# First stage of a two-layer decoder trunk: distance tables ahead of x, value and key/value weights split by ScalarE and VectorE, sinks on GpSimd

## Chip, cores and metric

One NeuronCore of a Trainium2 chip runs the whole program in one launch. The metric is device time in microseconds (us) of one execution; lower is better. The engines are PE (TensorE matmul; PEld is its weight load), DVE (VectorE), ACT (ScalarE), POOL (GpSimd) and SP (SyncE, which here only issues DMAs).

## What is computed

A trunk of two decoder layers on x of 512 tokens by 1024 channels, in float32. Only the first steps of layer 0 bear on this change:

```python
h = rms_norm(x, g_mix[layer])
proj = jnp.einsum("bsd,de->bse", h, w_in)
aq, ak, av, bq, bk, bv = jnp.split(proj, offs, axis=-1)
aq = rms_norm(aq.reshape(bsz, seq, N_HEADS_A, HEAD_DIM), a_q_gain)
...
a_out = dilated_attention(aq, ak, av, slopes[N_HEADS_B:])
b_out = sliding_window_sink_attention(bq, bk, bv, b_sinks, slopes[:N_HEADS_B])
```

The dilated attention (A, 8 heads) lets token t see the keys at distance 0 to 128, at multiples of 4 up to 512 and at multiples of 16 up to 2048; a key that is in several of these branches counts as often. The sliding window (B, 8 query heads, 2 key/value heads) sees 128 keys and a learned sink per head. Both subtract a slope times the distance. After attention come an output projection and a squared-ReLU MLP, and then layer 1 with another attention.

## The kernel before, in words

Every matmul is made in three products: each float32 operand is split into a high part (whi, h[:, 0]) and a residual (wlo, h[:, 1]), and high times high, residual times high and high times residual are summed in PSUM. A split of weights is one cast (L151 on ScalarE, L153 on GpSimd) and one subtraction (L156 on VectorE or GpSimd). Which engines do it is chosen by a pattern that a counter walks through: PAT_START is ScalarE with VectorE, PAT_ATT is GpSimd with VectorE and then GpSimd for both. The raw weights (wraw) have 4 buffers, whi and wlo 7 each.

A scheduler places the instructions of each engine in one order at build time; an engine runs its own in that order and waits on semaphores. Operations passed through in_order keep the order in which they are written while the start is emitted.

The first stage brings x in by halves. For each of 8 chunks of 128 channels, PE transposes x into a PSUM bank (xT, L629), ScalarE and VectorE write h times the gain and its residual (L160, L161), and ScalarE copies the transposed x to xs, of which GpSimd spills pairs of chunks to DRAM (L641). ScalarE also squares x (junk, L668) for the row statistics. Interleaved with this runs the projection of q and k of the first four A heads, project (L232 to L234), into four PSUM tiles pj0 to pj3. Four banks (pA) serve these projections and the two transposes of gains (pg).

norm_heads then copies each tile to SBUF (qk, L248; these share four buffers with xs), squares it (sq, L250), and VectorE sums the squares per head (ss, L251), takes reciprocal roots in small steps (rsqb, rsq, rs, L130 to L135) and multiplies (L261, shared with GpSimd). In layer 0 sq has a single buffer, which junk and the scratch f of the tables use as well. A PSUM bank is free once both copy and square have read it.

v_a(0) projects the values of the same four heads, 256 columns, 96 matmuls; prep_v scales and splits them (L160, L161). Then attention over A starts: PE transposes q and k (qkT, L268), ScalarE and VectorE split them (L278, L279, L160, L161), a DMA on SP swaps halves of K (L291), and scores follow. Interleaved with it run the projections for B: kv_b (256 columns of key and value) and then its queries.

make_tables builds the tables that scores add: dist, the distance; lt, the log of the number of branches; lb, the mask of B. It is emitted after all of the q and k projection. The sinks, negated (nsink, L679), are made on VectorE from a DMA that SP issues behind the weights and the gains.

Of the kernel before, what the change touches and what calls it, by code (L numbers as in the profile page):

```python
# [9 lines left out]
F32 = mybir.dt.float32  # L10
F32R = mybir.dt.float32r
BF16 = mybir.dt.bfloat16
I32 = mybir.dt.int32
# [60 lines left out]
def trunk(ctx, tc, x, g_mix, g_mlp, w_in_even, a_q_gain, a_k_gain, b_q_gain, b_k_gain, b_sinks,  # L74
# [118 lines left out]
    def layer_attention(li, hT, w_in, w_out, stats=None):  # L193


        with ExitStack() as c2:
# [41 lines left out]
                use(outs)  # L238
                yield 0

            def norm_heads(outs, nh):

                w = nh * HD
                qk = [ap.tile([P, 2, 512], F32, tag="qk", bufs=4, name="qk") for _ in range(2)]
                ss = small.tile([P, NT, 8], F32, tag="ss", name="ss")
                for t in range(NT):
                    q = qk[t // 2][:, t % 2, :w]
                    nc.scalar.copy(q, outs[t][:, :w])  # L248
                    sq = ap.tile([P, 512], F32, tag="sq", bufs=1 + li, name="sq")
                    nc.scalar.activation(sq[:, :w], outs[t][:, :w], AF.Square)  # L250
                    nc.vector.reduce_sum(ss[:, t, :nh], sq[:, :w].rearrange("p (h d) -> p h d", d=HD), axis=AX.X)  # L251
                v = small.tile([P, NT, 8], F32, tag="ssv", name="ssv")
                for t in range(NT):
                    nc.vector.tensor_scalar(v[:, t, :nh], ss[:, t, :nh], 1.0 / HD, ecol[:, t:t + 1],
                                            op0=OP.mult, op1=OP.add)
                rs = small.tile([P, NT, 8], F32, tag="rs", name="rs")
                rsqrt_small(rs[:, :, :nh], v[:, :, :nh])
                for t in range(NT):
                    q = qk[t // 2][:, t % 2, :w].rearrange("p (h d) -> p h d", d=HD)
                    eng = nc.gpsimd if NORM[t] == "g" else nc.vector  # L260
                    eng.tensor_mul(q, q, rs[:, t, :nh].unsqueeze(2).to_broadcast([P, nh, HD]))  # L261
                return qk
# [235 lines left out]
                    st["v", g] = prep_v(outs, 0, 4, i)  # L498
                return use

            def qk_use(key, nh):
                def use(outs):
                    st["qk", key] = norm_heads(outs, nh)
                return use

            def all_of(gen):
# [3 lines left out]
            if li == 0:  # L510
# [2 lines left out]
                                   *((PAT_START, True) if g == 0 else ()))  # L513

                def v_a(g):
                    return project([(1024 + g * 256, 1024 + g * 256 + 256)], v_use(g, 0))

                def att_a(g):
                    def get(p_):
# [4 lines left out]
                def kv_b():  # L524
                    def use(outs):
                        st["v", 3] = prep_v(outs, P, 2, 1)
                        st["k", "b"] = norm_heads(outs, 2)
                    return project([(2048, 2304)], use)

                def att_b():  # L530
                    def get(p_):
# [3 lines left out]
                        return prep_q(st["qk", "b"], p_ * P), [k, k]  # L535
                    return attend(get, 0, lambda: st["v", 3], lambda j: j // 4, "b", 0, 4, 4)

                first, qk0 = start(ap, hT), qk_a(0)
                for i, n in enumerate((1, 1 + 8 // GRAIN, 1 + 8 // GRAIN, 1 + 8 // GRAIN)):
                    cnt["start"] = i < STARTPIN  # L540
                    next(first)
                    for _ in range(n):
                        next(qk0)
                cnt["start"] = False
                for _ in range(8 // GRAIN):
                    next(qk0)
                next(first)
                all_of(qk0)
                make_tables(ap, dist, lt, lb)
                all_of(v_a(0))  # L550
                run(att_a(0), 32, chain(kv_b(), project([(1536, 2048)], qk_use("b", 8))), 768, LEADS[0])
                run(att_b(), NB, chain(qk_a(1), v_a(1)), 768, LEADS[1])
# [57 lines left out]
    def start(ap, hT):  # L610
# [65 lines left out]
                                bass.AP(tensor=g.tensor, offset=g.offset, ap=[[HD, 1], [0, 2], [1, HD]]))  # L676
        sink = small.tile([P, HA], F32, tag="sink", name="sink")
        nc.sync.dma_start(sink, bass.AP(tensor=b_sinks.tensor, offset=b_sinks.offset, ap=[[0, P], [1, HA]]))
        nc.vector.tensor_scalar_mul(nsink, sink, -1.0)  # L679
        nc.sync.dma_start(bfor, bass.AP(tensor=b_forget.tensor, offset=b_forget.offset, ap=[[0, P], [1, HC]]))  # L680
        nc.vector.tensor_add(ms[:, 0], ms[:, 0], ms[:, 1])
        col_stats(ms[:, 0])
# [4 lines left out]
    def make_tables(ap, dist, lt, lb):  # L687


        di = ap.tile([P, 512], I32, tag="bias", bufs=2, name="di")  # L690
        nc.gpsimd.iota(di, pattern=[[-1, 512]], base=384, channel_multiplier=1)
        nc.vector.tensor_copy(dist, di)
        mi = ap.tile([P, 512], I32, tag="bias", bufs=2, name="mi")
        mf = mi.bitcast(F32)
        f = ap.tile([P, 512], F32, tag="sq", bufs=1, name="f")
        nc.vector.tensor_scalar(lt, dist, 128.0, None, op0=OP.is_le)
        for m in (3, 15):
            nc.vector.tensor_scalar(mi, di, m, None, op0=OP.bitwise_and)
            nc.vector.tensor_scalar(f, mi, 0.0, None, op0=OP.is_equal)
            nc.vector.tensor_add(lt, lt, f)  # L700
        nc.vector.tensor_scalar(f, dist, 0.0, None, op0=OP.is_ge)
        nc.vector.tensor_mul(lt, lt, f)
        nc.vector.tensor_scalar(f, lt, 0.0, -8.0 * BIG, op0=OP.is_equal, op1=OP.mult)
        for n in (2, 3):
            nc.vector.tensor_scalar(mf, lt, float(n), float(8 * np.log(n)), op0=OP.is_equal, op1=OP.mult)
            nc.vector.tensor_add(f, f, mf)
        nc.vector.tensor_copy(lt, f)
        nc.vector.tensor_scalar(f[:, :256], dist[:, 256:], 0.0, -8.0 * BIG, op0=OP.is_lt, op1=OP.mult)
        nc.vector.tensor_scalar(lb, dist[:, 256:], 128.0, -8.0 * BIG, op0=OP.is_ge, op1=OP.mult)
        nc.vector.tensor_add(lb, lb, f[:, :256])  # L710

    def forget(ap, outs):

# [439 lines left out]
```

## Time and profile before

| | us |
|---|---|
| median of 3 runs | 1192.4 |
| lowest and highest run | 1188.94, 1193.04 |
| profiled execution, its own time | 1192.98 |
| span in its trace | 1191.2 |
| busy in the span: PE, PEld | 1162.3, 1020.3 |
| busy: VectorE, ScalarE, GpSimd | 893.1, 646.0, 212.1 |
| PE on the chain that ended last | 81% |

The span runs from the first to the last instruction; the execution's time has some 2 us around it. PE is busy for 98% of the span, so what counts is where PE waits, and for whom. A busy PE can still be slow: the granted clock says at which share of full speed it ran. A row of the timeline gives start, duration, engine, line, operation and tiles, and in brackets the idle time before it with what ended it. Durations of neighbours overlap a little, since instructions are pipelined; the distance between two starts is the better measure of a pace.

### The profile page before, as it was taken

What the parts mean: (1) busy time and instruction counts of PE and PEld (TensorE: products, weight loads), DVE (VectorE), ACT (ScalarE), POOL (GpSimd) and SP (SyncE); (2) the same over time, 40 slices, a digit from 0 to 9 for tenths busy, and PEclk for the clock granted to TensorE, in tenths of its full rate; (3) what the DMA queues carried; (4) which work ended last, traced back from release to release, by engine and by line L of the source; (5) the groups of instructions that cost most, each with busy time, mean ns of one, the idle gap of its engine ahead of it and who ended that gap; (6) DMA issues with size and microseconds to landing.
All of it is one profiled execution on the core that took longest, in us unless ns stands there. A gap on an engine that the chain in (4) does not pass through costs nothing.

```text
span 1191.2 us, 18927 instructions
## 1 busy us (share of the span) xinstructions
PE 1162.3 (98%) x6902; PEld 1020.3 (86%) x6902; DVE 893.1 (75%) x1962; ACT 646.0 (54%) x1351; POOL 212.1 (18%) x307
## 2 busy tenths in 40 slices
PE   8799989999999999999999999999999999999998
PEld 7787887888888988988887888887889989889897
DVE  4987899878956947865657887878879578569585
ACT  6255876665445545444335675655655455455453
POOL 2445444200000000000155445432000000000000
PEclk9899999999999999999999999999999999999999
DMA  7342115232332332233443433343322423323322
GB/s 250 114 109 79 37 37 155 76 103 75 107 110 84 94 120 88 90 113 109 152 125 107 106 100 100 103 124 106 107 89 72 125 89 106 103 83 100 116 68 82
DMA packets 106197, 122.46 MB, mean 103 GB/s; under 512 B 6088, under 2 KB 95208, under 8 KB 106104
## 3 DMA queue, kind: packets, MB, share of 16 engines
q1 hardware_dynamic: 104920, 117.03, 32.3%
q0 software_dynamic: 576, 2.10, 0.5%
q10 hardware_dynamic: 608, 2.13, 0.4%
q8 instruction: 54, 0.88, 0.3%
q14 instruction: 39, 0.32, 0.1%
HBM read 108.10 MB, written 6.32 MB: 96 GB/s over the span
## 4 chain that ended last, share of the span: by engine, by line
PE 81%; DVE 10%; DMA 3%; issue 2%; ACT 2%; POOL 1%; SPq 0%; ACTq 0%; POOLq 0%; DVEq 0%
PE up L165 10%; PE up L168 10%; PE up L169 10%; PE pj L232 4%; PE pj L234 4%; PE pj L233 4%; PE Y L950 3%; PE Y L953 3%; PE Y L954 3%; PE O L383 2%; PE Z L950 2%; PE X L953 2%; PE X L950 2%; PE Z L954 2%; PE Z L953 2%; PE X L954 2%
## 5 line engine op out<-in xcount | busy, mean ns | idle before, releaser
L165 PE MATMUL up<-xin,whi 128*128 128x512 f32 x512 | 199.8, 390 | 0.0
L168 PE MATMUL up<-xin,wlo 128*128 128x512 f32 x512 | 199.3, 389 | 0.0
L169 PE MATMUL up<-xin,whi 128*128 128x512 f32 x512 | 199.2, 389 | 0.0
L763 ACT CAST whi<-wraw 128x512 fp32r<-128x512 f32 (+1 forms) x228 | 138.7, 613 | 106.4 <-PE up L169 48.3
L764 DVE TENSOR_TENSOR wlo<-wraw,whi 128x512 fp32r<-128x512 f32 (+1 forms) x228 | 152.1, 679 | 56.5 <-ACT whi L763 54.3
L169 PEld LDWEIGHTS up<-xin,whi 128*128 128x128 f32 x512 | 96.1, 188 | 20.1
L165 PEld LDWEIGHTS up<-xin,whi 128*128 128x128 f32 x512 | 96.1, 188 | 20.0 <-issue 0.2
L168 PEld LDWEIGHTS up<-xin,wlo 128*128 128x128 f32 x512 | 96.1, 188 | 19.9 <-issue 0.2
L763 ACT CAST whi<-s 128x512 fp32r<-128x512 f32 (+1 forms) x112 | 67.6, 604 | 70.0 <-PE Y L954 35.0
L343 ACT ACTIVATE P<-P,negm 128x128 f32<-128x128 f32 (+5 forms) x128 | 69.5, 544 | 52.9 <-DVE negm L340 51.0
L950 PE MATMUL Y<-t,whi 128*128 128x256 f32 x324 | 92.7, 286 | 3.0 <-DVE acc L966 2.6
L901 ACT ACTIVATE u<-up 128x512 f32<-128x512 f32 x64 | 38.3, 598 | 99.7 <-PE up L169 99.7
L953 PE MATMUL Y<-t,wlo 128*128 128x256 f32 x324 | 91.7, 283 | 0.0
L954 PE MATMUL Y<-t,whi 128*128 128x256 f32 x324 | 91.6, 283 | 0.0
L153 POOL TENSOR_SCALAR whi<-wraw 128x512 fp32r<-128x512 f32 x96 | 65.8, 687 | 140.7 <-PE pj L234 118.3
L232 PE MATMUL pj<-whi,hn 128*128 128x512 f32 (+2 forms) x256 | 88.7, 346 | 0.0
L234 PE MATMUL pj<-whi,hn 128*128 128x512 f32 (+2 forms) x256 | 86.9, 339 | 0.0
L233 PE MATMUL pj<-wlo,hn 128*128 128x512 f32 (+2 forms) x256 | 86.8, 339 | 0.0
L764 DVE TENSOR_TENSOR wlo<-s,whi 128x512 fp32r<-128x512 f32 (+1 forms) x112 | 73.7, 663 | 2.4 <-ACT whi L763 2.4
L232 PE MATMUL pj<-whi,h 128*128 128x512 f32 (+1 forms) x192 | 68.5, 361 | 6.9 <-DVE v L161 3.1
L156 POOL TENSOR_TENSOR wlo<-wraw,whi 128x512 fp32r<-128x512 f32 x52 | 69.7, 1344 | 21.8 <-ACT whi L151 18.7
L234 PE MATMUL pj<-whi,h 128*128 128x512 f32 (+1 forms) x192 | 66.6, 348 | 0.0
(200 smaller groups left out, 3138.6 us busy)
## 6 DMA issues: line engine op xcount, KB each, us to landing
wraw<-in_w_up SPq DMA_DIRECT2D x64, 512.0 KB, 3.8
wraw<-in_w_down SPq DMA_DIRECT2D x58, 512.0 KB, 4.0
wraw<-in_w_in_odd SPq DMA_DIRECT2D x36, 256.0 KB, 3.0
K<-K SPq DMA_DIRECT2D x26, 256.0 KB
wraw<-in_w_in_even SPq DMA_DIRECT2D x10, 512.0 KB, 4.4
wraw<-in_w_in_even SPq DMA_DIRECT2D x16, 256.0 KB, 4.4
xl<-xsp SPq DMA_DIRECT2D x8, 512.0 KB
bias<-csp SPq DMA_DIRECT2D x16, 256.0 KB, 3.5
```

Source lines behind the costliest of these rows:

```text
L156: in_order((nc.gpsimd if lo == "pool" else nc.vector).tensor_sub(dst_l, src, dst_h.bitcast(F32)))
L165: m = nc.tensor.matmul(o, wh, xh, start=start, stop=False, skip_group_check=more)
L168: nc.tensor.matmul(o, wl, xh, start=False, stop=False, skip_group_check=more)
L169: nc.tensor.matmul(o, wh, xl, start=False, stop=stop, skip_group_check=more)
L232: nc.tensor.matmul(o, xh, hi[:, :n], start=k == 0, stop=False)
L233: nc.tensor.matmul(o, xh, lo[:, :n], start=False, stop=False)
L234: nc.tensor.matmul(o, xl, hi[:, :n], start=False, stop=k == DC - 1)
L763: sca(nc.scalar.copy(dst_h, src))
L764: late.append(lambda: vec(nc.vector.tensor_sub(dst_l, src, dst_h.bitcast(F32))))
L950: m = nc.tensor.matmul(o, wh, b(0), start=start, stop=False, skip_group_check=more)
L953: nc.tensor.matmul(o, wl, b(0), start=False, stop=False, skip_group_check=more)
L954: nc.tensor.matmul(o, wh, b(1), start=False, stop=stop, skip_group_check=more)
```

## The change

Four edits are in the diff. norm_heads and qk_use get parameters for the tag and the number of buffers of sq. The value projection of the first four A heads and the key/value projection of B take PAT_START. make_tables becomes a generator whose rows keep their written order: ten rows (dist to the first lt) are emitted before x, nine after the first pair of chunks; its scratch f moves from the buffer of sq to that of the probabilities P3. nsink is made by GpSimd.

```diff
-            def norm_heads(outs, nh):
+            def norm_heads(outs, nh, sq_tag="sq", sq_bufs=1 + li):
...
-                    sq = ap.tile([P, 512], F32, tag="sq", bufs=1 + li, name="sq")
+                    sq = ap.tile([P, 512], F32, tag=sq_tag, bufs=sq_bufs, name="sq")
...
-            def qk_use(key, nh):
+            def qk_use(key, nh, *sq):
                 def use(outs):
-                    st["qk", key] = norm_heads(outs, nh)
+                    st["qk", key] = norm_heads(outs, nh, *sq)
...
-                    return project([(1024 + g * 256, 1024 + g * 256 + 256)], v_use(g, 0))
+                    return project([(1024 + g * 256, 1024 + g * 256 + 256)], v_use(g, 0), PAT_START if g == 0 else PAT_ATT)
...
-                    return project([(2048, 2304)], use)
+                    return project([(2048, 2304)], use, PAT_START)
...
-                first, qk0 = start(ap, hT), qk_a(0)
+                tables, first, qk0 = make_tables(ap, dist, lt, lb), start(ap, hT), qk_a(0)
+                next(tables)
                 for i, n in enumerate((1, 1 + 8 // GRAIN, 1 + 8 // GRAIN, 1 + 8 // GRAIN)):
                     cnt["start"] = i < STARTPIN
                     next(first)
                     for _ in range(n):
                         next(qk0)
+                    if i == 0:
+                        next(tables)
...
-                make_tables(ap, dist, lt, lb)
...
-        nc.vector.tensor_scalar_mul(nsink, sink, -1.0)
+        nc.gpsimd.tensor_scalar(nsink, sink, -1.0, 1.0, op0=OP.mult, op1=OP.mult)
...
-        f = ap.tile([P, 512], F32, tag="sq", bufs=1, name="f")
-        nc.vector.tensor_scalar(lt, dist, 128.0, None, op0=OP.is_le)
+        f = scratch(F32, "P3", "f")
+        in_order(nc.vector.tensor_scalar(lt, dist, 128.0, None, op0=OP.is_le))
...
+        yield
...
```

The call of qk_use in qk_a and the one for B's queries are not in the diff: both still read qk_use(g, 8) and qk_use("b", 8).

Three places show what moves. The first is VectorE at the start of the program, before the change:

```order
L692 CAST dist_99<-di_464 128x512 [waits Pool_49]
L698 TENSOR_SCALAR mi_467<-di_464 128x512
L696 TENSOR_SCALAR lt_100<-dist_99 128x512 [waits DVE_49]
L709 TENSOR_SCALAR lb_101<-dist_99 128x256
L624 COPY gcol_83<-pg_140 128x16 [waits PE_49]
L161 SCALAR_TENSOR_TENSOR h0_0_148<-xT_143,gcol_83,h0_0_148 128x512 [waits Activation_49]
L161 SCALAR_TENSOR_TENSOR h0_1_156<-xT_151,gcol_83,h0_1_156 128x512 [waits Activation_49]
L156 TENSOR_TENSOR wlo_167<-wraw_163,whi_166 128x512 [waits DMAHW4_49,DMAHW3_49,Activation_49]
```

and with it, from the last of the first ten table rows on:

```order
L707 TENSOR_TENSOR lt_100<-lt_100,f_110 128x512 [waits DVE_49]
L626 COPY gcol_83<-pg_154 128x16 [waits PE_49]
L161 SCALAR_TENSOR_TENSOR h0_0_162<-xT_157,gcol_83,h0_0_162 128x512 [waits Activation_49]
L161 SCALAR_TENSOR_TENSOR h0_1_170<-xT_165,gcol_83,h0_1_170 128x512 [waits Activation_49]
L156 TENSOR_TENSOR wlo_181<-wraw_177,whi_180 128x512 [waits DMAHW4_49,DMAHW3_49,Activation_49]
L156 TENSOR_TENSOR wlo_185<-wraw_177,whi_184 128x512 [waits Activation_49]
L709 TENSOR_SCALAR f_110<-lt_100 128x512
L711 TENSOR_SCALAR mi_109<-lt_100 128x512
L712 TENSOR_TENSOR f_110<-f_110,mi_109 128x512 [waits DVE_49]
L711 TENSOR_SCALAR mi_109<-lt_100 128x512 [waits DVE_49]
L712 TENSOR_TENSOR f_110<-f_110,mi_109 128x512 [waits DVE_49]
L713 COPY lt_100<-f_110 128x512 [waits DVE_49]
```

Behind the iota's cast three table rows stood ahead of the gains' copy; now nine do, and the other nine stand between the residuals of the first two chunks' weights and the third chunk (three of them below the piece shown).

The second is ScalarE at the end of the first q and k projection, from the last square of x on; "waits" names the engine whose semaphore is awaited. Before:

```order
L668 ACTIVATE junk_385,ms0_135<-x3_109 128x512 [waits Activation_49]
L248 COPY qk_421<-pj0_159 128x512 [waits DMASW0_49,PE_49]
L250 ACTIVATE sq_425<-pj0_159 128x512 [waits Activation_49]
L248 COPY qk_421<-pj1_160 128x512 [waits PE_49]
L250 ACTIVATE sq_429<-pj1_160 128x512 [waits DVE_49]
L248 COPY qk_422<-pj2_161 128x512 [waits DMASW1_49,PE_49]
L250 ACTIVATE sq_433<-pj2_161 128x512 [waits DVE_49]
L248 COPY qk_422<-pj3_162 128x512 [waits PE_49]
L250 ACTIVATE sq_437<-pj3_162 128x512 [waits DVE_49]
L160 ACTIVATE v0_102<-pj0_487,rcol_94 128x4x64 [waits PE_49]
```

and with the change:

```order
L670 ACTIVATE junk_408,ms0_149<-x3_123 128x512 [waits Activation_49]
L248 COPY qk_444<-pj0_173 128x512 [waits DMASW0_49,PE_49]
L250 ACTIVATE sq_448<-pj0_173 128x512 [waits Activation_49]
L248 COPY qk_444<-pj1_174 128x512 [waits PE_49]
L151 CAST whi_555<-wraw_549 128x512
L250 ACTIVATE sq_452<-pj1_174 128x512 [waits DVE_49]
L248 COPY qk_445<-pj2_175 128x512 [waits DMASW1_49,PE_49]
L151 CAST whi_621<-wraw_619 128x512 [waits DMAHW2_49]
L248 COPY qk_445<-pj3_176 128x512 [waits PE_49]
L250 ACTIVATE sq_456<-pj2_175 128x512 [waits DVE_49]
L151 CAST whi_625<-wraw_619 128x512
L151 CAST whi_753<-wraw_751 128x512 [waits DMAHW3_49]
```

The casts of the value weights and of B's key/value weights, which GpSimd made, stand among the head copies and squares; each square after the first still waits for VectorE.

The third is VectorE from the end of the reciprocal roots to the last v residual. Before:

```order
L135 SCALAR_TENSOR_TENSOR rs_445<-rsq_447,rsq_446 128x32 [waits DVE_49]
L161 SCALAR_TENSOR_TENSOR v0_102<-pj0_487,rcol_94,v0_102 128x4x64 [waits Activation_49]
L261 TENSOR_TENSOR qk_421<-qk_421,rs_445 128x512 [waits DMASW0_49,DVE_49]
L261 TENSOR_TENSOR qk_422<-qk_422,rs_445 128x512 [waits DMASW1_49]
L705 TENSOR_SCALAR mi_467<-lt_100 128x512
L161 SCALAR_TENSOR_TENSOR v0_102<-pj1_488,rcol_94,v0_102 128x4x64 [waits Activation_49]
L706 TENSOR_TENSOR f_468<-f_468,mi_467 128x512 [waits DVE_49]
L161 SCALAR_TENSOR_TENSOR v0_102<-pj2_489,rcol_94,v0_102 128x4x64 [waits Activation_49]
L707 COPY lt_100<-f_468 128x512 [waits DVE_49]
L156 TENSOR_TENSOR wlo_910<-wraw_903,whi_909 128x512 [waits DMAHW4_49,Pool_49]
L708 TENSOR_SCALAR f_468<-dist_99 128x256 [waits DVE_49]
L161 SCALAR_TENSOR_TENSOR v0_102<-pj3_490,rcol_94,v0_102 128x4x64 [waits Activation_49]
```

and with the change:

```order
L135 SCALAR_TENSOR_TENSOR rs_468<-rsq_470,rsq_469 128x32 [waits DVE_49]
L261 TENSOR_TENSOR qk_444<-qk_444,rs_468 128x512 [waits DMASW0_49,DVE_49]
L261 TENSOR_TENSOR qk_445<-qk_445,rs_468 128x512 [waits DMASW1_49]
L161 SCALAR_TENSOR_TENSOR v0_102<-pj0_487,rcol_94,v0_102 128x4x64 [waits Activation_49]
L161 SCALAR_TENSOR_TENSOR v0_102<-pj1_488,rcol_94,v0_102 128x4x64 [waits Activation_49]
L161 SCALAR_TENSOR_TENSOR v0_102<-pj2_489,rcol_94,v0_102 128x4x64 [waits Activation_49]
L156 TENSOR_TENSOR wlo_910<-wraw_903,whi_909 128x512 [waits DMAHW4_49,Pool_49]
L161 SCALAR_TENSOR_TENSOR v0_102<-pj3_490,rcol_94,v0_102 128x4x64 [waits Activation_49]
```

The table rows (L705 to L708) are gone from between the q/k products and the v residuals; the products now stand ahead of all four v residuals, and one weight residual ahead of the fourth. After the first two heads of the attention the orders of all engines are the same as before.

## Rows read from the trace of the kernel before

**Rows 1.** Windows: stretch, length, busy PE, PEld, DVE, ACT, POOL, clock, DMA share, GB/s.
```profile
35.30:58.95 23.65, 17.46 (x116) 16.28 (x117) 21.76 (x48) 5.23 (x10) 10.90 (x10) 0.88 0.26 70
```

**Rows 2.** Waits of PE, 0 to 60 us: total, times, longest.
```profile
PE pj L232 <- DVE v L161: 3.1, 3, 2.4
...
PE pj L232 <- POOL wlo L156: 2.3, 1, 2.3
```

**Rows 3.** Timeline of PE: start, us, engine, line, op, out<-in [idle before it <-releaser].
```profile
35.05 0.24 PE L623 MATMUL pg<-ident,rows 22*128 22x22 f32 x1
...
52.09 0.28 PE L233 MATMUL pj<-wlo,h 128*128 128x256 f32 x1
52.21 0.28 PE L234 MATMUL pj<-whi,h 128*128 128x256 f32 x1
...
58.89 0.41 PE L268 MATMUL qkT<-ident,qk 128*128 128x128 f32 x1
```

**Rows 4.** Windows, three short stretches (columns as in rows 1).
```profile
41.00:43.00 2.00, 2.00 (x12) 2.00 (x11) 1.81 (x8) 0.00 (x0) 0.00 (x0) 0.52 0.67 183
58.00:60.00 2.00, 1.92 (x9) 1.92 (x10) 1.64 (x4) 0.66 (x1) 0.00 (x0) 0.50 0.72 205
112.00:116.00 4.00, 2.66 (x14) 1.64 (x12) 3.64 (x6) 0.59 (x1) 3.27 (x3) 1.00 0.91 260
```

**Rows 5.** Timeline of ScalarE, 23 to 38 us.
```profile
23.38 0.63 ACT L668 ACTIVATE junk<-x 128x512 f32<-128x512 f32 x1
...
24.14 0.63 ACT L668 ACTIVATE junk<-x 128x512 f32<-128x512 f32 x1
...
25.91 1.14 ACT L151 CAST whi<-wraw 128x512 fp32r<-128x512 f32 x2
26.94 1.08 ACT L639 COPY xs<-xT 128x512 f32<-128x512 f32 x2
...
36.81 0.60 ACT L250 ACTIVATE sq<-pj 128x512 f32<-128x512 f32 x1 [3.79 <-DVE ss L251]
```

**Rows 6.** Timeline of VectorE, 28 to 59 us.
```profile
28.67 2.76 DVE L681 TENSOR_TENSOR ms<-ms 128x4 f32<-128x4 f32 x1
...
41.18 0.42 DVE L699 TENSOR_SCALAR f<-mi 128x512 f32<-128x512 int32 x1
...
47.60 1.27 DVE L135 SCALAR_TENSOR_TENSOR rsq<-rsq 128x32 f32<-128x32 f32 x1
...
49.58 0.17 DVE L134 TENSOR_TENSOR rsq<-rsq 128x32 f32<-128x32 f32 x1
...
50.79 2.86 DVE L261 TENSOR_TENSOR qk<-qk,rs 128x512 f32<-128x512 f32 x2
...
57.55 0.47 DVE L161 SCALAR_TENSOR_TENSOR v<-pj,rcol,v 128x256 fp32r<-128x256 f32 x1
57.95 0.41 DVE L710 TENSOR_TENSOR lb<-lb,f 128x256 bf16<-128x256 bf16 x1
```

**Rows 7.** Timeline of GpSimd, one row.
```profile
28.95 1.29 POOL L156 TENSOR_TENSOR wlo<-wraw,whi 128x512 fp32r<-128x512 f32 x1
```

**Rows 8.** Timeline of VectorE, first 23 us.
```profile
2.49 0.43 DVE L692 CAST dist<-di 128x512 f16<-128x512 int32 x1 [0.50 <-POOL di L691]
...
5.04 0.17 DVE L624 COPY gcol<-pg 128x16 f32<-128x16 f32 x1 [1.32 <-PE pg L623]
...
12.27 1.28 DVE L156 TENSOR_TENSOR wlo<-wraw,whi 128x512 fp32r<-128x512 f32 x2
20.62 0.17 DVE L679 TENSOR_SCALAR nsink<-sink 128x8 f32<-128x8 f32 x1 [7.06 <-DMA sink<-in_b_sinks]
```

**Rows 9.** Timeline of PE in the dense first stage.
```profile
12.29 0.40 PE L233 MATMUL pj<-wlo,h 128*128 128x512 f32 x1
...
17.95 0.40 PE L233 MATMUL pj<-wlo,h 128*128 128x512 f32 x1
```

**Rows 10.** The spills of x, line 641: time from issue to landing.
```profile
DMA to landing us min/median/max: 3.8/5.2/6.9
```

More of the change, by code (lines that the diff above doesn't have):

```diff
@@ L687, in make_tables, with scratch @@
     def make_tables(ap, dist, lt, lb):
-        di = ap.tile([P, 512], I32, tag="bias", bufs=2, name="di")
+        def scratch(dt, tag, name):
+            return ap.tile([P, 512], dt, tag=tag, bufs=2, name=name)
+        di = scratch(I32, "bias", "di")
         nc.gpsimd.iota(di, pattern=[[-1, 512]], base=384, channel_multiplier=1)
-        nc.vector.tensor_copy(dist, di)
-        mi = ap.tile([P, 512], I32, tag="bias", bufs=2, name="mi")
+        in_order(nc.vector.tensor_copy(dist, di))
+        mi = scratch(I32, "bias", "mi")
@@ L694, in make_tables @@
         mf = mi.bitcast(F32)
-        f = ap.tile([P, 512], F32, tag="sq", bufs=1, name="f")
-        nc.vector.tensor_scalar(lt, dist, 128.0, None, op0=OP.is_le)
+        f = scratch(F32, "P3", "f")
+        in_order(nc.vector.tensor_scalar(lt, dist, 128.0, None, op0=OP.is_le))
         for m in (3, 15):
[L698 to L701, printed above, removed]
@@ L702, in make_tables @@
-        nc.vector.tensor_mul(lt, lt, f)
-        nc.vector.tensor_scalar(f, lt, 0.0, -8.0 * BIG, op0=OP.is_equal, op1=OP.mult)
-        for n in (2, 3):
[L705 to L709, printed above, removed]
@@ L710, in make_tables @@
-        nc.vector.tensor_add(lb, lb, f[:, :256])
+            in_order(nc.vector.tensor_scalar(mi, di, m, None, op0=OP.bitwise_and))
+            in_order(nc.vector.tensor_scalar(f, mi, 0.0, None, op0=OP.is_equal))
+            in_order(nc.vector.tensor_add(lt, lt, f))
+        in_order(nc.vector.tensor_scalar(f, dist, 0.0, None, op0=OP.is_ge))
+        in_order(nc.vector.tensor_mul(lt, lt, f))
+        yield
+        in_order(nc.vector.tensor_scalar(f, lt, 0.0, -8.0 * BIG, op0=OP.is_equal, op1=OP.mult))
@@ new lines, in make_tables @@
+        for n in (2, 3):
+            in_order(nc.vector.tensor_scalar(mf, lt, float(n), float(8 * np.log(n)), op0=OP.is_equal, op1=OP.mult))
+            in_order(nc.vector.tensor_add(f, f, mf))
+        in_order(nc.vector.tensor_copy(lt, f))
+        in_order(nc.vector.tensor_scalar(f[:, :256], dist[:, 256:], 0.0, -8.0 * BIG, op0=OP.is_lt, op1=OP.mult))
+        in_order(nc.vector.tensor_scalar(lb, dist[:, 256:], 128.0, -8.0 * BIG, op0=OP.is_ge, op1=OP.mult))
+        in_order(nc.vector.tensor_add(lb, lb, f[:, :256]))
@@ L712, in forget @@
+        yield
     def forget(ap, outs):
```

## Prediction

> **What bounds the kernel now.** I read the windows by stage first, then the waits of PE, then the timelines of PE, ScalarE and VectorE over the first 60 us. PE is the bound nearly everywhere. The exception that this change can reach is one stretch. From 35.30 to 58.95 us, the first value projection and the hand-over to attention, PE is busy 17.46 of 23.65 us at a mean granted clock of 0.88, while VectorE is busy 21.76 [rows 1]. The waits name above all GpSimd's residual of the value weights (2.3) and VectorE's residual of v (3.1 in three waits, one of 2.4) [rows 2]. The timeline gives the edges: the transpose that ends the dense first stage starts at 35.05 and lasts 0.24, so I count from 35.3; the last value matmul starts at 52.21; the last transpose of q and k starts at 58.89, and I count it to 58.95 [rows 3]. [...] Dense at the upper level a 128x256 matmul follows the last after 0.12 us (52.09 to 52.21 [rows 3]).
>
> **Term 1, the value projection.** It has 96 matmuls, 11.5 us dense, and now ends at 52.3. Its first matmul needs two things: weights and a PSUM bank. The weights came from GpSimd; split by ScalarE and VectorE they are ready near 30, because ScalarE has little to do then. The bank needs the square of the second q/k tile. That square waited 3.79 us, until 36.81, for VectorE's reduction of the first [rows 5], because VectorE sat from 28.67 for 2.76 us in a 128x4 addition while GpSimd made a residual from 28.95 to 30.24 [rows 6, 7]; that work leaves GpSimd here.
>
> The title of the change says two buffers for the squares. The diff does not deliver them: norm_heads and qk_use take a tag and a count, but no caller passes any, so layer 0 keeps one buffer, and the ScalarE order still shows each square from the second on waiting for VectorE. That edit costs and brings nothing, and I count on one buffer.
>
> ScalarE's order: the spill copies of the last chunk end at 28.0 now (26.94 + 1.08) [rows 5]; three of the four squares of x that ran before them move behind, so about 27.1. Then four such squares at 0.76 (23.38 to 24.14) and three casts at 0.57 (1.14 for two) [rows 5] put the first head copy at 31.9. Copy and square end at 33.0, VectorE reduces by 34.0, the second square ends at 34.7: PE starts at once, at 35.3. Its second bank waits for VectorE's copy of the gains, now ahead of the third reduction, about 36.6: 1.3 us idle. The third square ends near 37.0, the fourth near 39.4, when PE has used up 23 of its matmuls: 0.2 idle. End 35.3 + 11.5 + 1.5 = 48.3; I take 48.5, since every link is a sum of rows without slack. **Term 1: -3.8.** Bounds: dense, 46.8 (-5.5); releases and lower clock as now, with only the weights early, 51.2 (-1.1). I take a value nearer the first because 1.5 us of idle is close to what 112 to 116 shows at full clock [rows 4].
>
> Moved to VectorE are four 128x512 residuals (0.64 each, 1.28 for two [rows 8]), to ScalarE eight casts; ScalarE is busy 5.23 us of this stretch [rows 1], so those are covered.
>
> **Term 2, from the last value matmul to the last transpose.** Today 52.3 to 58.95, 6.6 us. The reason is VectorE: 15 table rows, the first at 41.18 and the last at 57.95 [rows 6], some 8 us, lie between the reciprocal roots, the q/k products and the v residuals that PE waits for. They leave. VectorE's new order from the fourth reduction (41.0): a weight residual, then eleven small rows at about 0.2 (0.17 and a gap, 49.58 [rows 6]) = 2.2, plus 1.1 because GpSimd's remaining split falls on them (such a row took 1.27 at 47.60 [rows 6]), so the roots are ready at 45.2. Two products in 2.86 (50.79 [rows 6]) end at 48.0, three v residuals at 0.47 at most (57.55 [rows 6]) end near 49.2, and one weight residual later the fourth ends at 50.2. PE arrives at 48.5 and finds all but the fourth: 12 matmuls (1.4) and 8 transposes (0.6), with 0.5 waiting, 2.5 us. **Term 2: -4.1.** Bounds: no wait at all, -4.7; the new waits described in the second rival, -2.0.
>
> **Term 3.** With no gap there the lower clock of 58 to 60 [rows 4] falls away; from 58.95 on it cost about half of 1 us: **-0.5**, bounds 0 and -0.5.
>
> **The start, costed at nothing.** VectorE gets ten table rows before the gains and nine between the first two chunk pairs. Ten rows from 2.49 (seven at 0.43, three of two inputs like a residual's 0.64) end near 7.5, so the gains' copy moves from 5.04 to 7.5 [rows 8]; x's first halves then leave ScalarE by 8.9, the weights' residual VectorE by 10.4, and PE wants that at 12.29 [rows 9]. The second batch and one bias row, 4.5 us from 11.0, put the second pair's weight residual at 17.5; PE now wants it at 17.95 [rows 9], and the new PE order puts three more matmuls ahead of it. The cover is VectorE's 7.06 us wait for the sinks' DMA, until 20.62 [rows 8], which goes to GpSimd. If that cover were a microsecond short, PE would idle that microsecond, inside a dense run. Behind the sinks on GpSimd wait the second and later spills, not wanted before 34.7.
>
> After two heads of attention the orders of all engines are the same again, so the shift should carry through. The q and k splits, K's copy DMA and the first scores hang on the last transpose and move with it; on SP a weight load now stands between the two copies of K, behind a residual that VectorE makes before the second K anyway.
>
> **Sum.** -3.8 - 4.1 - 0.5 = -8.4 against the profiled execution's 1192.98, 1184.6. The median of the three runs is 0.6 lower, 1192.4; I forecast the median, 1184.0. The bounds add to -3.1 and -10.7: 1189.3 and 1181.7.
>
> **Rivals.**
> [...]
> 2. *VectorE's queue is the new wait.* It runs in order. A weight residual now stands before the roots and waits for a ScalarE cast, which waits for PE to let a buffer go; another stands before the fourth v and waits for a GpSimd cast. For: both stand in the new order. Against: PE frees both buffers before VectorE gets there, if terms 1 and 2 hold. If both bite, term 2 is -2.0 and term 1 -2.5: 1187.4.
> 3. *Given back later.* Were VectorE the pace of the attention stage, PE would arrive early and wait. Against: its rows start earlier too. Half the sum lost: 1188.2.
> 4. *Slower: the spills.* The third head copy writes a buffer whose old content the second spill must have sent. That spill now stands behind the sinks' row, issued near 21 instead of 14, landing 3.8 to 6.9 us later [rows 10], by 28, wanted at 34.7. For: spills and table rows now share the same microseconds. Against: the four spills landed within 6.9 in the trace, and the second batch of table rows ends near 15.6, before the second spill is issued. Each microsecond beyond 34.7 is one on PE's path, and from 43.1 on the kernel is slower than before; landing at 50 would give 1199.3. [...]
>
> **How the numbers follow.** Forecast 0.60, rival 1 0.16, rival 2 0.12, rival 3 0.08, rival 4 0.04. A measurement here tells 0.5%, 6.0 us, from no change: faster means under 1186.4. That is nearly all of the forecast (0.56), half of rival 1 (0.09) and a little of rival 2 (0.02): 0.67. Slower is rival 4, 0.04; the rest, 0.29, is the same. The range takes the bounds of the sum, widened downward by the spread of single runs: 1181.0 to 1189.5; what it leaves out is rival 4, ends of rival 3 and runs beyond the lower end.
>
> **What would show it.** Right: the first value matmul at about 35.3 without a wait on GpSimd; the projection's end near 48.5; no table row on VectorE after 20 us; last q/k transpose near 51; granted clock 1.00 from 41 to 60; PE dense from 10.5 to 35 as before; one square at a time, each after VectorE's reduction. [...]

## The result and the profile after

The changed kernel takes 1183.61 us (median of 6 runs, 1182.03 to 1184.7) against 1191.95 of the kernel before beside it (6 runs, 1188.94 to 1194.19): ratio 0.993, interval 0.9915 to 0.9945. The forecast was 1184.0, and 8.3 us less is more than the 6.0 us (0.5%) from which the prediction called a change faster. Repeated in two later sets on two chips, the same kernel came to 0.9926 and 0.9925, which is 9.4 and 9.8 us between the medians. The profiled execution took 1184.7 us with a span of 1182.9 (before 1192.98 and 1191.2), so its 8.3 us can be looked for in the spans.

Windows of the changed kernel, the stretch of [rows 1] and two of [rows 4]; columns as there.

```profile
35.30:58.95 23.65, 22.94 (x182) 21.95 (x180) 19.34 (x52) 10.31 (x24) 10.79 (x12) 1.00 0.46 132
41.00:43.00 2.00, 2.00 (x19) 2.00 (x18) 1.83 (x7) 0.00 (x0) 0.52 (x1) 1.00 0.66 203
58.00:60.00 2.00, 1.40 (x12) 1.22 (x12) 1.40 (x5) 1.72 (x6) 1.64 (x3) 1.00 0.43 137
```

PE is busy 22.94 of 23.65 us instead of 17.46, at a granted clock of 1.00 instead of 0.88. VectorE has gone from 21.76 to 19.34, and PE waits for it far less, as the next view shows.

Waits of PE in the first 60 us of the changed kernel, to be read against [rows 2].

```profile
...
PE xT L631 <- DMA x<-in_x: 2.0, 1, 2.0
PE pj L232 <- DVE v L161: 0.7, 1, 0.7
PE S L326 <- DVE bias L307: 0.6, 1, 0.6
```

GpSimd's residual of the weights (2.3) is gone, VectorE's residual of v is down from 3.1 to 0.7. New is 0.6 for a bias row of VectorE at the second head's scores; in the two later profiles of the same kernel 0.3 for K's copy stands there instead.

Timeline of PE in the changed kernel, the edges of [rows 3].

```profile
36.20 0.24 PE L625 MATMUL pg<-ident,rows 22*128 22x22 f32 x1
36.37 0.38 PE L232 MATMUL pj<-whi,h 128*128 128x256 f32 x1
...
47.86 0.28 PE L234 MATMUL pj<-whi,h 128*128 128x256 f32 x1
47.98 0.28 PE L232 MATMUL pj<-whi,h 128*128 128x256 f32 x1
...
50.03 0.38 PE L232 MATMUL pj<-whi,h 128*128 128x256 f32 x1 [0.70 <-DVE v L161]
...
50.49 0.93 PE L268 MATMUL qkT<-ident,qk 128*128 128x128 f32 x7
...
56.29 0.28 PE L326 MATMUL S<-K,Q 128*128 128x256 f32 x1
```

The value projection runs from 36.37 to 47.98 without one gap: 11.6 us for 96 matmuls. 3.2 us later the last transpose is done (51.17), and the first score of attention starts at 56.29; in the kernel before it started at 64.64. These 8.35 us are the whole difference of the spans (8.3): what comes later carries them through.

What VectorE and GpSimd do in the changed kernel, for [rows 6] and [rows 8].

```profile
32.29 0.16 DVE L683 TENSOR_TENSOR ms<-ms 128x4 f32<-128x4 f32 x1
36.48 0.18 DVE L626 COPY gcol<-pg 128x22 f32<-128x22 f32 x1 [0.32 <-PE pg L625]
44.60 0.19 DVE L135 SCALAR_TENSOR_TENSOR rs<-rsq 128x32 f32<-128x32 f32 x1
49.50 0.47 DVE L161 SCALAR_TENSOR_TENSOR v<-pj,rcol,v 128x256 fp32r<-128x256 f32 x1
```

```profile
20.67 0.19 POOL L681 TENSOR_SCALAR nsink<-sink 128x8 f32<-128x8 f32 x1 [8.54 <-DMA sink<-in_b_sinks]
20.88 0.58 POOL L643 DMA_DIRECT2D xsp<-xs  x1
...
42.48 0.61 POOL L153 TENSOR_SCALAR whi<-wraw 128x512 fp32r<-128x512 f32 x1 [13.40 <-PE pj L234]
```

The small addition of squares that took 2.76 us beside GpSimd rows takes 0.16; GpSimd has no row of compute from 20.86 to 42.48. The wait for the sinks is GpSimd's now, and no wait of PE hangs on what stands behind it.

### The profile page after: what moved, and what is told of

Read it like the earlier page. It is cut to its first block, busy times and chain, and to the rows that moved or that the text cites. A ratio compares the mean times of both kernels' runs of the same rounds, so it can differ in the third digit from the quotient of the medians.

```text
span 1182.9 us, 18918 instructions
## 1 busy us (share of the span) xinstructions
PE 1160.1 (98%) x6902; PEld 1018.8 (86%) x6902; DVE 889.7 (75%) x1965; ACT 649.2 (55%) x1359; POOL 202.0 (17%) x296
## 4 chain that ended last, share of the span: by engine, by line
PE 75%; DVE 6%; DMA 1%; ACT 1%; issue 1%; POOL 0%; ACTq 0%; DVEq 0%; POOLq 0%
PE up L165 10%; PE up L168 10%; PE up L169 10%; PE Y L957 3%; PE Y L960 3%; PE Y L961 3%; PE pj L234 3%; PE pj L232 3%; PE pj L233 3%; PE Z L957 2%; PE X L960 2%; PE X L957 2%; PE X L961 2%; PE Z L960 2%; PE Z L961 2%; PE O L383 2%
## 5 line engine op out<-in xcount | busy, mean ns | idle before, releaser
L771 DVE TENSOR_TENSOR wlo<-wraw,whi 128x512 fp32r<-128x512 f32 (+1 forms) x228 | 152.2, 679 | 56.5 <-ACT whi L770 56.5
L153 POOL TENSOR_SCALAR whi<-wraw 128x512 fp32r<-128x512 f32 x88 | 60.6, 690 | 142.8 <-PE pj L234 122.0
L156 POOL TENSOR_TENSOR wlo<-wraw,whi 128x512 fp32r<-128x512 f32 x48 | 63.9, 1334 | 21.0 <-ACT whi L151 18.3
L156 DVE TENSOR_TENSOR wlo<-wraw,whi 128x512 fp32r<-128x512 f32 (+1 forms) x76 | 53.7, 714 | 17.9 <-POOL whi L153 9.8
L232 PE MATMUL pj<-whi,h 128*128 128x512 f32 (+1 forms) x192 | 66.5, 353 | 0.7 <-DVE v L161 0.7
```

Of the source, the lines that this page charges most:

```text
L156: in_order((nc.gpsimd if lo == "pool" else nc.vector).tensor_sub(dst_l, src, dst_h.bitcast(F32)))
L232: nc.tensor.matmul(o, xh, hi[:, :n], start=k == 0, stop=False)
L771: late.append(lambda: vec(nc.vector.tensor_sub(dst_l, src, dst_h.bitcast(F32))))
```

## The experiments

One trap had to be cleared first: the second gains transpose, which ends the dense first stage, does not start at the same time in two executions of one kernel. So I read each profile by the distance from that transpose to the first score, and give it beside the time. In three profiles of the changed kernel that distance is 20.09, 20.08 and 20.08, with the transpose at 36.20, 34.71 and 35.86. The distance leaves out what PE loses before that transpose; where there is such a wait (e4, e7, e9), the text names it.

| kernel | transpose | first score | between | median us (runs) | ratio to before |
|---|---|---|---|---|---|
| before | 35.05 | 64.64 | 29.59 | 1191.95 to 1193.61 | 1 |
| changed | 36.20 | 56.29 | 20.09 | 1183.61 (6) | 0.993 [0.9915, 0.9945] |
| e5_after | 34.71 | 54.79 | 20.08 | 1183.96 (6) | 0.9926 [0.9911, 0.9941] |
| e12_after | 35.86 | 55.94 | 20.08 | 1183.80 (5) | 0.9925 [0.9908, 0.9942] |
| e1_weights | 35.17 | 57.81 | 22.64 | 1187.47 (5) | 0.9948 [0.9934, 0.9963] |
| e2_tables | 36.18 | 58.98 | 22.80 | 1186.62 (5) | 0.9946 [0.9933, 0.9959] |
| e4_sink_dve | 40.84 | 60.92 | 20.08 | 1190.22 (12) | 0.998 [0.997, 0.999] |
| e8_kvb_att | 34.80 | 57.80 | 23.00 | 1185.95 (6) | 0.9942 [0.9928, 0.9957] |
| e9_kvb_dve | 34.10 | 54.95 | 20.85 | 1184.23 (6) | 0.9929 [0.9911, 0.9947] |
| e7_tables_two | 36.28 | 57.84 | 21.56 | 1186.12 (6) | 0.9946 [0.9931, 0.9962] |
| e6_two | 34.65 | 54.55 | 19.90 | 1182.18 (6) | 0.992 [0.9902, 0.9937] |
| e3_late | 35.21 | 54.56 | 19.35 | 1182.36 (4) | 0.991 [0.9896, 0.9924] |
| e10_late | 34.70 | 54.05 | 19.35 | 1182.38 (5) | 0.9915 [0.9896, 0.9934] |
| e11_late_two | 34.65 | 54.53 | 19.88 | 1183.21 (5) | 0.992 [0.9902, 0.9937] |

e1 to e4, e5 to e8 and e9 to e12 each ran on one chip; times are compared within such a group, distances across all.

**The weights alone (e1_weights).** On the kernel before:

```
-  return project([...], v_use(g, 0))
+  return project([...], v_use(g, 0), PAT_START if g == 0 else PAT_ATT)
-  return project([(2048, 2304)], use)
+  return project([(2048, 2304)], use, PAT_START)
```

> Only the weights' pattern of the first value projection and of the block-B key and value projection is changed; tables and sinks stay as in the kernel before. Theory A (the prediction's terms 1 and 2 are separate and add up): the last value matmul comes at about 48.5 us instead of 52.3, so 3.8 us less, 1188.2 us. Theory B (VectorE, 21.76 us busy of 23.65 in that stretch, is the one bound of it, and the table rows and the heads' products still stand in it): the value matmuls end earlier, but the last query and key transpose still waits for VectorE, which has got two weight rows of 0.68 more; 1191.5 to 1193.5 us, with the last transpose still at 58 us or later.

1187.47, 5.3 us less than the kernel before beside it. Theory B fell, and A was short: the distance is 6.95 us less.

Timeline of VectorE, e1_weights.

```profile
45.91 0.48 DVE L161 SCALAR_TENSOR_TENSOR v<-pj,rcol,v 128x256 fp32r<-128x256 f32 x1
...
48.54 0.48 DVE L161 SCALAR_TENSOR_TENSOR v<-pj,rcol,v 128x256 fp32r<-128x256 f32 x1
...
51.18 0.47 DVE L161 SCALAR_TENSOR_TENSOR v<-pj,rcol,v 128x256 fp32r<-128x256 f32 x1
```

Between the four value residuals (the third is at 50.00) the table rows still stand, and PE waits 1.7 us for them in three pieces. But they stand there some six microseconds earlier than before: the fourth was at 57.55 [rows 6].

**The tables and sinks alone (e2_tables).** The changed kernel with those two patterns taken back:

```
-  return project([...], v_use(g, 0), PAT_START if g == 0 else PAT_ATT)
+  return project([...], v_use(g, 0))
-  return project([(2048, 2304)], use, PAT_START)
+  return project([(2048, 2304)], use)
```

> Tables early and sinks on GpSimd as in the changed kernel; both weight patterns stay as before. Theory A: term 2 and the clock (4.1 + 0.5) less the 1.1 us that the first stage lost in the changed kernel: 1188.4 us, last value matmul at 52 to 53.5 us, last transpose some 2.5 us behind it. Theory B (VectorE alone is the bound): nearly the whole gain, 1183.5 to 1185 us. Together with the first run this gives the interaction: under A the two gains add up to that of the whole change (8.3), under B they do not.

1186.62, 6.15 us less, distance 6.79 less. Each half alone wins about 6.9 of the 9.5 that both win, so they overlap by 4.2. Neither theory had it: they don't add, and neither half is the whole. Here the first wait of PE in the projection is for a square, and the granted clock of the stretch is 0.87. The run holds the tables' new place, their fixed order and the other buffer of f together; only the sinks were tried singly.

Timeline of PE, e2_tables, and the window from 35.3 to 48 us.

```profile
38.44 0.42 PE L232 MATMUL pj<-whi,h 128*128 128x256 f32 x1 [1.34 <-ACT sq L250]
```

```profile
35.30:48.00 12.70, 11.27 (x74) 10.29 (x73) 10.56 (x32) 3.22 (x6) 5.86 (x6) 0.87 0.34 108
```

**The sinks back on VectorE (e4_sink_dve).** On the changed kernel:

```
-  nc.gpsimd.tensor_scalar(nsink, sink, -1.0, 1.0, op0=OP.mult, op1=OP.mult)
+  nc.vector.tensor_scalar_mul(nsink, sink, -1.0)
```

> The changed kernel with the sinks' negation back on VectorE. The prediction's theory: VectorE stands at that row for its transfer (7.06 us in the kernel before), but has nothing that PE waits for behind it there: within 0.5 us of the changed kernel, 1183.1 to 1184.2. Rival: with 20 rows of tables ahead of it in that stretch the wait is no longer covered and holds the residuals behind it; a listed wait of PE on VectorE between 20 and 30 us and 1185 or more.

1190.22, and the rival holds: the wait comes where it said. Timeline of VectorE, then of PE, e4_sink_dve.

```profile
18.80 0.17 DVE L681 TENSOR_SCALAR nsink<-sink 128x8 f32<-128x8 f32 x1 [5.10 <-DMA sink<-in_b_sinks]
...
20.61 1.40 DVE L161 SCALAR_TENSOR_TENSOR h<-xT,gcol,h 128x512 fp32r<-128x512 f32 x2
21.93 1.28 DVE L156 TENSOR_TENSOR wlo<-wraw,whi 128x512 fp32r<-128x512 f32 x2
```

```profile
22.67 0.49 PE L233 MATMUL pj<-wlo,h 128*128 128x512 f32 x1 [3.73 <-DVE wlo L156]
...
23.46 0.63 PE L234 MATMUL pj<-whi,h 128*128 128x512 f32 x1
```

In the order of VectorE the sinks' row stands amid the second batch of table rows. It waits 5.10 us for its transfer, and the residuals of h and of the weights, which PE needs, queue behind it. Soon after its 3.73 us without work PE falls to half pace, 0.43 us from start to start from 23.46 to 26.45, which is the other part of the price. From the second gains transpose on the kernel is the changed one again: the distance is 20.08. In the kernel before the same row waited 7.06 us [rows 8] and cost nothing: the second pair's residuals (12.27 [rows 8]) stood ahead of it, and PE has no wait between 12.5 and 35. So early tables need the sinks elsewhere; by the medians that row is worth some 6.4 us here (against 1183.8, the changed kernel's median on another chip). The profile is the fastest of the twelve runs, 1187.29; its stage ends 4.6 to 6.1 us later than in the three profiles of the changed kernel.

**The block-B weights back (e8_kvb_att).** On the changed kernel:

```
-  return project([(2048, 2304)], use, PAT_START)
+  return project([(2048, 2304)], use)
```

> The changed kernel with the block-B key and value weights back on the pattern of before (GpSimd and VectorE). Theory A (GpSimd, which holds two heads' products of 2.95 us from 44.9 on, gets four more rows for weights that PE needs in the same time): 0.4 to 1.5 us slower than the changed kernel beside it, with a wait of PE on GpSimd between 51 and 60 us. Theory B (this projection fills gaps of attention and its weights are early enough either way): within 0.4 us.

2.0 us slower than the changed kernel beside it, distance 2.9 more. Slower, as theory A has it, but by more than its 1.5 and in another place: PE doesn't wait for GpSimd between 51 and 60, it waits at 38 for the gains' copy.

Timelines of PE, GpSimd and VectorE, e8_kvb_att, and the window from 35.3 to 48 us.

```profile
38.18 0.39 PE L232 MATMUL pj<-whi,h 128*128 128x256 f32 x1 [1.88 <-DVE gcol L626]
```

```profile
31.49 1.29 POOL L156 TENSOR_TENSOR wlo<-wraw,whi 128x512 fp32r<-128x512 f32 x1
34.28 1.71 POOL L153 TENSOR_SCALAR whi<-wraw 128x512 fp32r<-128x512 f32 x2 [1.50 <-PE pj L234]
36.07 1.26 POOL L156 TENSOR_TENSOR wlo<-wraw,whi 128x512 fp32r<-128x512 f32 x1
```

```profile
31.65 1.16 DVE L141 TENSOR_SCALAR ecol<-msv 128x4 f32<-128x4 f32 x1
...
36.52 0.83 DVE L133 SCALAR_TENSOR_TENSOR rsq<-msv,rsq 128x4 f32<-128x4 f32 x1
37.28 0.68 DVE L156 TENSOR_TENSOR wlo<-wraw,whi 128x512 fp32r<-128x512 f32 x1
...
37.95 0.17 DVE L626 COPY gcol<-pg 128x22 f32<-128x22 f32 x1
```

```profile
35.30:48.00 12.70, 10.82 (x78) 10.61 (x77) 9.77 (x29) 2.52 (x5) 5.87 (x6) 0.87 0.43 125
```

VectorE's rows of 4 columns, 0.16 in the changed kernel, take up to 1.16 beside GpSimd's rows; its order also puts a second weight residual (37.28) before the gains' copy. That comes 3.15 us after its transpose (34.80) instead of 0.28 us. The wait of 1.88 us is not all of the 2.9: the clock of the stretch is 0.87 and not 1.00, and from 39.41 to 42.61 the matmuls follow each other after 0.21 instead of 0.12 us, some 1.4 us (an estimate, 15 matmuls); the 0.7 for the fourth value residual, on the other hand, are gone.

**The same weights all on VectorE (e9_kvb_dve)** tells GpSimd's presence from VectorE's load:

```
-  return project([(2048, 2304)], use, PAT_START)
+  return project([(2048, 2304)], use, (("dve", "dve"),))
```

> The changed kernel with both parts of the block-B key and value weights on VectorE: GpSimd stays as empty from 28 to 40 us as in the changed kernel, VectorE gets four rows of about 0.42 us more. Theory A (in the run with these weights on GpSimd it is GpSimd's rows beside VectorE's that stretched those and made the second gains' copy 3.0 us late): the gains' copy comes within 0.6 us of its transpose, PE waits for it under 0.5 us, and the time is within 0.8 us of the changed kernel run beside it. Theory B (what decides is how much work VectorE has before the gains' copy, whatever GpSimd does): PE waits 1 to 2 us for the gains' copy or a square, and the time is 1.5 to 2.5 us above the changed kernel, as in that run.

1184.23, 0.4 us over the changed kernel beside it. Timeline of VectorE, e9_kvb_dve.

```profile
32.59 0.42 DVE L155 CAST whi<-wraw 128x512 fp32r<-128x512 f32 x1
...
34.48 0.15 DVE L133 SCALAR_TENSOR_TENSOR rsq<-msv,rsq 128x4 f32<-128x4 f32 x1
34.55 0.17 DVE L626 COPY gcol<-pg 128x22 f32<-128x22 f32 x1
```

With more work on VectorE and none on GpSimd the copy comes 0.45 us after its transpose (34.10), and PE doesn't wait for it. Theory A holds, with one reserve: in this order the second weight residual (0.68) stands behind the copy, so that much of e8's delay can be order and not GpSimd. PE does wait 1.1 instead of 0.7 for the fourth value residual, half of the 0.77 us that the distance is longer. The profiled execution is the slowest of the six, 1187.11; its first 60 us show no reason, and I leave that open.

**Two buffers for the squares, really passed (e7_tables_two, e6_two).** On e2_tables and on the changed kernel:

```
-  return project([...], qk_use(g, 8),
+  return project([...], qk_use(g, 8, *(("P2", 2) if g == 0 else ())),
```

> The run with tables early and both weight patterns as before (1186.6 us, PE waiting 1.3 us for a square at 38.44 and a granted clock of 0.87 from 35.3 to 48), now with two buffers for the first squares. Theory A (there the one buffer is a real wait): the 1.3 us go, the clock stays up, 1184.5 to 1185.5 us. Theory B (GpSimd's weight rows of 1.26 to 1.30 us, on which the kernel before waited 2.3 us, come in its place): PE waits for a wlo of GpSimd instead, 1186.0 to 1187.0.

> The changed kernel with two buffers really passed to the first heads' squares. Theory A (PE waits for no square there any more, 0 of 13.2 us): within 0.5 us of the changed kernel run beside it. Theory B (the squares, one at a time from 32.7 to 40 us, hold the root of the norms and through it the heads' products and the fourth value residual, for which PE waits 0.7 us): up to 0.7 us faster, the root's last step before 44.0 us instead of 44.6.

Timeline of PE, e7_tables_two, and the window from 35.3 to 48 us.

```profile
30.51 0.50 PE L233 MATMUL pj<-wlo,h 128*128 128x512 f32 x1 [1.58 <-DVE wlo L156]
...
39.36 0.38 PE L232 MATMUL pj<-whi,h 128*128 128x256 f32 x1 [1.95 <-DVE gcol L626]
```

```profile
35.30:48.00 12.70, 10.75 (x84) 10.09 (x83) 11.24 (x32) 2.99 (x6) 6.62 (x7) 1.00 0.48 160
```

In e7 the 1.3 us for the square go, as A said. But in its place PE waits 1.95 us for the gains' copy, and not for GpSimd's residual, as B said. That the distance is 1.24 less all the same comes with the clock, which reads 1.00 from 35.3 to 48 here and 0.87 in e2. Before the transpose PE loses 1.58 us to a weight residual of VectorE, which the distance doesn't count. The time, 1186.12, lies in B's range, but neither theory had this course. An idle of 1.95 us left the clock up here, one of 1.88 in e8 did not (0.87 over the same stretch): what decides is open, and so part of e8's price may be chance. On the changed kernel (e6) the second buffer brings the roots of the norms forward from 8.39 to 6.96 us after the transpose, and PE still waits 0.5 instead of 0.7: 0.18 us of distance. The medians differ by 1.8, but the runs of e6 lie in two groups, 1181.65 to 1182.32 and 1184.3 to 1185.55, and with late tables the second buffer makes the distance 0.53 us longer (e11; 0.8 between the medians, with overlapping runs). A gain from it is not shown.

**The changed kernel again (e5_after, e12_after).**

> The changed kernel unaltered, as a standard for the other runs on this chip. Ratio to the kernel before 0.993, as before; S of the first head at about 56.3 us and the second gains transpose at about 36.2 us again, if these belong to the order and not to one execution; if the late start is chance, the second gains transpose comes anywhere from 35.0 to 36.3.

> The changed kernel unaltered, the standard of this call. 1183 to 1184.5 us; the second gains transpose at 34.7 or at 36.2 us, with the gains' first copy at 7.52 us either way, if the moment at which the clock rises in the first stage is chance.

Chance it is, and wider than I gave it: the transpose comes at 34.71 in e5_after, earlier than its range, and at 35.86 in e12_after, at neither of the two times named. Timeline of PE, first of the changed kernel's first profile, then of e5_after: the same program, with the gains' copy at 7.52 and 7.53.

```profile
10.86 2.05 PE L232 MATMUL pj<-whi,h 128*128 128x512 f32 x4
12.71 0.63 PE L233 MATMUL pj<-wlo,h 128*128 128x512 f32 x1
13.14 0.63 PE L234 MATMUL pj<-whi,h 128*128 128x512 f32 x1
...
13.99 0.50 PE L234 MATMUL pj<-whi,h 128*128 128x512 f32 x1
14.33 0.40 PE L233 MATMUL pj<-wlo,h 128*128 128x512 f32 x1
```

```profile
10.41 1.71 PE L232 MATMUL pj<-whi,h 128*128 128x512 f32 x4
11.95 0.40 PE L233 MATMUL pj<-wlo,h 128*128 128x512 f32 x1
12.19 0.39 PE L234 MATMUL pj<-whi,h 128*128 128x512 f32 x1
```

In the first the matmuls follow each other after 0.43 us until 14, in the second after 0.23 from 11.95 on. The stage ends 1.5 us apart: 0.45 us by the start of the first matmul (10.86 and 10.41), the rest by the pace.

**Tables later (e3_late, e10_late, e11_late_two).** On the changed kernel; e11 adds the two buffers.

```
   tables, first, qk0 = make_tables(...), start(...), qk_a(0)
-  next(tables)
...
-      if i == 0:
+      if i < 2:
           next(tables)
```

> The changed kernel, with the first ten table rows moved behind the first pair of chunks and the rest behind the second pair. Theory A (the first ten rows hold the gains' copy from 5.0 to 7.5 us, and PE starts its matmuls later and at half pace for 1.7 us longer): the gains' copy is back at 5.0 us, the second gains transpose at about 35.05 us instead of 36.20, and the time is 1182.5 us. Theory B (x's transfer and the moment at which the clock rises set that, not the table rows): second gains transpose between 35.8 and 36.5, time 1183.3 to 1184.2. Theory C (rows moved to 16 to 25 us now hold the residuals that PE's dense first stage reads): a listed wait of PE on VectorE before 36 us, time 1184.5 or more.

> Tables behind the first and the second pair of chunks, again, now beside the changed kernel. Theory A (the late second gains transpose of the first profile was chance, and this order gains only what it won between that transpose and the first score, 19.35 us against 20.08): 0.4 to 1.2 us faster than the changed kernel. Theory B (the 1182.4 us of the first try were the draw of that chip): within 0.3 us of the changed kernel.

> Tables late and two buffers for the first squares together. Theory A (the last wait of PE on a value residual is gone with late tables already, so the second buffer has nothing left to win): within 0.4 us of the run with late tables alone. Theory B (both orders win separately): 0.2 to 0.8 us below it, under 1182 us.

Late tables give 1182.36, and again 1182.38 beside 1183.80 of the changed kernel: 1.4 us less, more than the 1.2 that A of e10 allowed, and with five runs each only the slowest of them lies within the changed kernel's spread (1182.12 to 1183.55 against 1183.41 to 1184.66). By the ratio to the kernel before it is the fastest version tried (10.4 and 11.2 us below it), though the intervals of the ratios overlap, e6's too. What A of e3 expected of the first gains' copy came (5.04 and 5.00 instead of 7.52), but it is not shown to be what helps: the stage's end, 35.21 and 34.70, lies within the changed kernel's own scatter. The wait that C expected did not come. Shown is half of the gain, 0.73 us of distance: PE waits for no value residual any more. The other half is open.

Windows of e10_late.

```profile
35.30:48.00 12.70, 12.70 (x106) 12.49 (x105) 10.49 (x28) 4.18 (x9) 6.63 (x7) 1.00 0.37 116
48.00:52.00 4.00, 4.00 (x35) 4.00 (x35) 2.51 (x4) 2.43 (x4) 1.82 (x2) 1.00 0.43 131
```

PE is busy without a break up to 52 us, so from the projection to there no wait is left for a further edit. e11 fits neither of its theories: PE waits 0.5 us for a value residual again, and the median came out 0.8 higher.

## Why the prediction was right

The time came within 0.4 us of the forecast. The mechanism held: PE no longer waits for GpSimd's weights, and VectorE's value residuals come before PE needs them but for one. The sizes of the steps held less exactly, with errors of both signs, so that the sum came so close is in part luck: beside 8.4 forecast, the medians give 8.3 here and 9.4 and 9.8 in the two later sets, and the distance gives 9.5.

- **Term 1, -3.8.** It gave the projection 13.2 us, from 35.3 to 48.5; it took 11.6, with not one idle gap. The 1.3 us for the gains' copy were wrong here: the copy came 0.28 after its transpose. I had put the copy late in VectorE's queue; with no GpSimd rows beside it the queue gets there in time, and ScalarE's first head copy, which I had at 31.9, starts at 30.74 in e5. Where GpSimd keeps its rows (e8), the idle is real, 1.88 us. The term is mis-sized by 1.6 us, its upper bound (dense) was the truth. One reading was off, too: the matmul at 52.21 already belongs to the next projection, for ScalarE takes the finished fourth value tile at 52.17. The value projection of the kernel before ends at 51.97; 0.36 us of term 1 belong to term 2, and the sum stays. Timeline of ScalarE, kernel before:

```profile
52.17 0.47 ACT L160 ACTIVATE v<-pj,rcol 128x256 fp32r<-128x256 f32 x1 [0.96 <-PE pj L234]
```

- **Term 2, -4.1.** From the last value matmul to the last transpose I gave 2.5 us, and it took 3.2: the wait was 0.7 and not 0.5, and the 12 matmuls and 8 transposes took 2.5 and not 2.0. Mis-sized by 0.7 the other way.
- **Term 3, -0.5.** The clock stays at 1.00 from 58 to 60, where it was 0.50. From the start of the last transpose to the first score it was 5.75 us (58.89 to 64.64, 0.41 of it that transpose), from its end at 51.17 it is 5.12 now: 0.2 to 0.6 less, which fits and can't be read closer.
- **The start, nothing.** No wait of PE stands between 10.5 and 35, as forecast, although the gains' copy came at 7.52. In the profile the stage still ends 1.15 us later, which I had not foreseen; the same program ends it at 34.71 in e5, so one execution does not show a loss. It hid the surplus of term 1: in that one execution -9.5 in the distance and +1.15 give the 8.35. The cover is thin, though: in e7 and e9, where full pace is there at 10.66 and 10.65 already, PE waits 0.3 us for the second pair's weight residual. Timeline of PE, e9_kvb_dve:

```profile
17.55 0.50 PE L233 MATMUL pj<-wlo,h 128*128 128x512 f32 x1 [0.32 <-DVE wlo L156]
```

- **Edits taken for terms.** I had hung term 1 on the weights and term 2 on the tables. e1 and e2 show that each edit alone shortens both pieces: from the transpose to the end of the value projection the weights win 4.3 us and the tables 1.7, from there to the last transpose 2.3 and 4.5 (both together 5.1 and 3.8). The weights take away GpSimd rows that lengthened VectorE's (2.76 us for an addition that takes 0.16 without them), the tables take away rows of VectorE. They overlap by 4.2 of 13.7 us. That did not enter the sum, because I had followed PE's timeline with all edits in place, not the edits one by one.
- **The sinks** I named as the cover's condition only; e4 shows it is worth some 6.4 us.
- **The inert edit** is inert: PE waits for no square in the changed kernel, and really passing two buffers (e6) shows no gain.
- **Rivals.** The first (the one buffer leaves PE idle in pieces, and the clock falls) did not come: PE waits for no square, and the clock reads 1.00 from 35.3 to 58.95. It stands in e2, where the weights stay with GpSimd (1.34 us for a square, 0.87 from 35.3 to 48), and its lower clock in e8 (0.87). The second is the 0.7 us. The third did not come: the 8.35 us are still there at the end. The fourth fell: spills landed 5.4 to 6.7 us after issue against 3.8 to 6.9 [rows 10], the second was issued at 20.88 as forecast, and ScalarE's copies waited for none.

## What to carry to other kernels

Work out a change on the timeline of the engine that sets the end, with all its edits in place: a sum over edits counts an overlap twice when they relieve the same engine. Before an in-order engine gets more work early, look for the row in it that waits for a transfer and move that row too; here it turned 9 us of gain into 2.5. An engine with room may still be the wrong place: rows of GpSimd off the path lengthened rows of VectorE on it (up to 1.16 us instead of 0.16, e8), and the same work was nearly free on the busier engine (0.4 us, e9).

## What was not expected of the hardware

- A VectorE addition of 128x4 took 2.76 us, to 31.43, beside a GpSimd residual [rows 6, 7] and the two casts behind it, which end at 31.41; without them it took 0.16. In e8 rows of 0.15 to 0.17 took up to 1.16. With more VectorE work and no GpSimd rows (e9) they took 0.15 to 0.17 again. In e8 the row of 1.16 ends at 32.81 and GpSimd's residual beside it at 32.78. What holds such a row is not shown, and why the addition lasted over three GpSimd rows and not one is open. Timeline of GpSimd, kernel before:

```profile
30.21 1.20 POOL L153 TENSOR_SCALAR whi<-wraw 128x512 fp32r<-128x512 f32 x2
```

- In the changed kernel's first profile the granted clock reads 1.00 in a stretch where the matmuls go at half pace; in e5_after it reads 0.72, and the matmuls go at full pace from 11.95 on. Window from 8.5 to 14 us, first of the changed kernel, then of e5_after:

```profile
8.50:14.00 5.50, 5.02 (x16) 3.95 (x17) 5.36 (x10) 4.74 (x9) 0.77 (x1) 1.00 1.05 364
```

```profile
8.50:14.00 5.50, 5.48 (x21) 4.44 (x22) 5.35 (x10) 4.75 (x9) 0.77 (x1) 0.72 1.04 358
```

  So the start-to-start distance of matmuls (0.43 or 0.23 us at 128x512) is the surer sign of the pace.
- The first row at full pace came between 10.65 and 14.77 us in nine profiles with early table rows, between 11.87 and 12.88 in the five others. Whether early rows widen that scatter is open; too few profiles were taken.
